# Mixer ends and the spread of the row scales in a three-block transformer kernel

## The chip, the cores and the metric

The kernel runs on one core of a Trainium2 chip, as one program and one launch. The metric is the device time of that launch in microseconds; before the change it is 1496.61 us, the median of three runs (1496.16 to 1496.88). The core has five engines with a queue of instructions each: TensorE (PE) multiplies matrices into PSUM banks, VectorE (DVE) and ScalarE (ACT) work elementwise and read PSUM, GpSimd (POOL) works elementwise on SBUF, and SyncE (SP) here only issues transfers.

## The reference, cut to what matters

256 tokens of width 1024 pass through two transformer layers of one kind and one of another, all in float32. Each of the first two layers is a feed-forward, a mixer (stick-breaking attention beside a convolution in the first layer, gated linear attention in the second) and another feed-forward; then comes a block with sparse attention, retention and a last feed-forward.

```python
for l in range(2):
    f = swiglu(rms_norm(h, g[0]), ffn1_w_in[l], ffn1_w_out[l])
    h = h + 0.5 * rms_norm(f, g[1])
    hn = rms_norm(h, g[2])
    m = even_mixer(hn, ...) if l % 2 == 0 else odd_mixer(hn, ...)
    h = h + rms_norm(m, g[3])
    f = swiglu(rms_norm(h, g[4]), ffn2_w_in[l], ffn2_w_out[l])
    h = h + 0.5 * rms_norm(f, g[5])
```

with `swiglu(x, w_in, w_out)`: split `x @ w_in` into `a` and `b`, then `(silu(a) * b) @ w_out`. A norm scales each token's row by the inverse root of its mean square, and each feature by a gain.

## The kernel before, in words

**Stages.** The program runs eight stages in a row: feed-forward, even mixer, feed-forward, feed-forward, odd mixer, feed-forward, the second block and its feed-forward. The loop over `i` (L1559) runs the first six. The 256 tokens are two tiles of 128 rows; `h` keeps both in SBUF. Between two stages stands `boundary` (L508): the last products of a stage for token tile 0, then for tile 1, and under those of tile 1 the next stage's input for tile 0 (transposes of `h` on TensorE, L409, then split columns `xh` and `xl`, L435 and L436). The transposes for tile 1 are put inside the next stage's first projection.

**Products in two parts.** Every float32 factor is split into a high half `hi` (a ScalarE copy, L248) and a low half `lo` (a subtraction, L249, mostly on VectorE), and each product is three matmuls: high by high (L271), low by high (L272) and high by low (L273). Nearly all weights come in chunks of 512 KB, in one fixed plan. `feed_dma` sends a chunk's transfer from SyncE into one of four `raw` buffers; `feed_cv` makes its halves. The transfer of chunk n + 4 goes into the buffer that the low half of chunk n sets free.

**What sets the order.** Nothing is scheduled: each engine works through its instructions in the order in which the code writes them. `nxt` hands out a chunk and first writes conversions ahead, up to one more than the chunks used, until they are `depth` ahead. `catch_up(n, lo_on)` writes up to n further conversions, with the low halves on VectorE or, with `pool`, on GpSimd. The tuples `PRE`, `PRT`, `PRF` and `CU` say how many of these stand at which place of `boundary`: the first two numbers ahead of tile 0's norm (on VectorE, on GpSimd), the third behind it (on GpSimd), then `CU[1]` behind tile 0's columns and `CU[2]` behind tile 0's scale (both on VectorE). `PRT` is for the two mixers, `PRF` for the four feed-forwards of the loop, `PRE` for the second block.

**Norms.** `add_normed` adds a stage's normed output to `h`: sums of squares on ScalarE (L359), then `rsqrt1` on 128x1 tiles of VectorE (L331 to L337), then for each half a gain (L374) and an addition (L380). `Lazy` keeps the next norm's row scales apart: `scale` makes them on GpSimd, and `rows` spreads them along the free axis: ScalarE puts each tile's scales on a diagonal `dg` (L448), TensorE multiplies by ones (L449), VectorE copies the result to `rb` (L451).

**A mixer's last projection.** `sproj_tail` makes it in four row blocks of the contraction: `part()` does the next one for both token tiles and both halves of the columns, `part(LO)` leaves out the two halves of tile 1, which `pieces()` then adds to the work of `boundary`. Each such piece is six matmuls.

**A feed-forward.** For 256 hidden features at a time (`j` from 0 to 10), `fa` and `fb` are projected, `sg = silu(fa * rb)` and `u = sg * fb` formed, `u` split into `hh` and `hl` (L550, L551), and the products with `fo` of the group before are added up (`fpart`). Group 0 has tokens on partitions, so that its `u0` is transposed (L739) in round `j = 1`, behind the spread.

Of the kernel before, what the change touches and what calls it, by code (L numbers as in the profile page):

```python
# [18 lines left out]
D = 1024  # L19
# [13 lines left out]
PRE = (1, 1, 2)  # L33
PRT = (0, 0, 2)
PRF = (0, 0, 2)
CT, CS = (2, 2), (0, 1)
CU = (2, 0, 1, 2)
# [143 lines left out]
class Norm:  # L181
    """a normalised activation on its way into the projections: split transposed columns and row scales"""
# [8 lines left out]
def block_kernel(ctx: ExitStack, tc: tile.TileContext, a: dict, out: bass.AP, upto: int = 99):  # L191
# [61 lines left out]
    def nxt(*names, ahead=True):  # L253
        """the next chunks; whatever uses the chunks before them is emitted already"""
        i = pos["use"]
        for d_, nm in enumerate(names):
            assert plan[i + d_][0] == nm, (plan[i + d_][0], nm)
        n = i + len(names)
        feed_cv(max(n, min(i - 1 + pos["depth"], pos["cv"] + len(names) + 1)) if ahead else n)
        pos["use"] += len(names)  # L260
        for _ in names:
            for f in list(side):
                f()
        r = [cv_t.pop(i + d_) for d_ in range(len(names))]
        return r if len(r) > 1 else r[0]

    def catch_up(n, lo_on=dve):
        feed_cv(min(pos["use"] - 1 + pos["depth"], pos["cv"] + n), lo_on)
# [56 lines left out]
    def rsqrt1(eng, ss, m, neps):  # L325
        """2^m / sqrt(ss[:, 0] + ss[:, 1] + neps)"""
        v = sm.tile([128, 1], F32, tag="rs_v", name="rs_v")
        vh = sm.tile([128, 1], F32, tag="rs_h", name="rs_h")
        y = sm.tile([128, 1], F32, tag="rs_y", name="rs_y")
        t = sm.tile([128, 1], F32, tag="rs_t", name="rs_t")  # L330
        eng.tensor_scalar(v, ss[:, 0:1], ss[:, 1:2], neps, op0=ALU.add, op1=ALU.add)  # L331
        eng.tensor_scalar(y.bitcast(I32), v.bitcast(I32), -0.5, float(MAGIC + (m << 23)), op0=ALU.mult, op1=ALU.add)
        if eng is dve:
            dve.tensor_scalar(vh, v, 0.5 * 4.0 ** -m, None, op0=ALU.mult)
            for _ in range(3):
                dve.scalar_tensor_tensor(t, in0=y, scalar=vh, in1=y, op0=ALU.mult, op1=ALU.mult)  # L336
                dve.scalar_tensor_tensor(y, in0=t, scalar=1.5, in1=y, op0=ALU.subtract, op1=ALU.mult, reverse0=True)  # L337
        else:
            pool.tensor_scalar(vh, v, -0.5 * 4.0 ** -m, None, op0=ALU.mult)
            for _ in range(3):  # L340
                pool.tensor_tensor(t, y, y, op=ALU.mult)
                pool.tensor_scalar(t, t, vh, 1.5, op0=ALU.mult, op1=ALU.add)  # L342
                pool.tensor_tensor(y, y, t, op=ALU.mult)
        return y

    def rsqrtn(v, n, big=False):
        """1 / sqrt(v), v: [128, n]"""
        mk = (lambda nm: s2([128, n], name=nm)) if big else (lambda nm: sm.tile([128, n], F32, tag=nm, name=nm))
        y, t = mk("rn_y"), mk("rn_t")
        dve.tensor_scalar(y.bitcast(I32), v.bitcast(I32), -0.5, float(MAGIC), op0=ALU.mult, op1=ALU.add)  # L350
        for _ in range(3):
            dve.scalar_tensor_tensor(t, in0=y, scalar=0.5, in1=y, op0=ALU.mult, op1=ALU.mult)
            dve.tensor_tensor(t, t, v, op=ALU.mult)
            dve.scalar_tensor_tensor(y, in0=t, scalar=1.5, in1=y, op0=ALU.subtract, op1=ALU.mult, reverse0=True)
        return y
# [11 lines left out]
    def add_normed(t, f, gb, m, rin=None):  # L367
        """h[:, t] += c * rms_norm(rin * f) * gb, c sqrt(D) = 2^m"""
# [24 lines left out]
    def add_gated(t, f, g):  # L393
        """h[:, t] += f * g"""
        for i in range(2):
            hv = h[:, t, i * 512:(i + 1) * 512]
            tm = s2([128, 512], name="tm")
            dve.tensor_tensor(tm, f[i], g[:, i * 512:(i + 1) * 512], op=ALU.mult)
            dve.tensor_tensor(hv, hv, tm, op=ALU.add)
            if i == 0:  # L400
                yield
# [9 lines left out]
    class Lazy:  # L411
        """x = h * r * g: columns of h * g, the row scales r apart"""
# [30 lines left out]
        def rows(self):  # L443
            """r along the free axis, in all partitions"""
            p = pb()
# [7 lines left out]
    class Shifted:  # L453
        """x = h * r * g + shift, whole"""
# [20 lines left out]
        def spread(self, t=0):  # L475
            """r along the free axis, in all partitions"""
# [30 lines left out]

    def boundary(pieces, fin, nz, pre=(0, 0, CU[0])):  # L508
        """the last products of a stage for token tile 0, then 1; the next stage's input for tile 0 under them"""
# [21 lines left out]
        catch_up(CU[1])  # L531
# [5 lines left out]
    def rows_T(t, src, xh, xl, halves=(0, 1)):  # L537
        """src [128 tokens, D] -> split transposed columns"""
# [15 lines left out]
    def wproj2(o, chs, x):  # L554
        """features on partitions, two tiles in one bank: o[:, i*256:] = (128 columns i of w)^T x^T"""
# [24 lines left out]
    def sproj(o, name, xh, xl, nk=8):  # L580
        """tokens on partitions: o(t) [128, 512] = x w, both token tiles chunk by chunk"""
# [5 lines left out]
    def sproj_ab(o, name, xh, xl, nk=8, mid=None):  # L587
        """the same, token tile 0 whole before 1"""
# [12 lines left out]
    def sproj_tail(name, xh, xl):  # L601
        """a projection to D columns, in four row blocks; part() does the next of them, pieces() the rest in boundary()"""
# [8 lines left out]
        def part(leave=()):  # L611
            """leave: (token tile, half) that wait for pieces()"""
# [47 lines left out]
    def ada_sum():  # L660
        """the four groups of 32 partitions together, and the columns to their places"""
# [8 lines left out]
    def gate_row(c0):  # L670
        """mod columns c0..c0+8 along the free axis, in all partitions: the tile and the work for its halves"""
# [12 lines left out]
    def ffn(nz, each=None):  # L684
# [45 lines left out]
        for j in range(1, NJ):  # L730
            if each and j > 1:
                each()
            pa = wp("fa", x)
            if j == 1:
                nz.rows()
# [6 lines left out]
            chb = nxt("fb", "fb")  # L742
# [6 lines left out]
            pb_ = pb()  # L749
            wproj2(pb_, chb, x)  # L750
# [24 lines left out]
    def even_mixer(nz):  # L775
# [91 lines left out]
        def logits(hp, pz, last):  # L867
            """masked, columns: keys 0..127 of all queries, then keys 128..255 of the later queries"""
# [108 lines left out]
        part()  # L977
        return f, pieces()

# [1 line left out]
    def odd_mixer(nz):  # L981
# [71 lines left out]
        def gate_sums():  # L1053
            """cs: sums within blocks of 64; last: the decay to the end of tile 0 and from the start of tile 1"""
# [12 lines left out]
        def halves(z, n):  # L1067
            """the lower and the upper blocks of n of each pair, all heads"""
# [8 lines left out]
        def decay(l):  # L1077
            """blocks of n = 64 >> l: the decay up to the end of the lower ones and from the start of the upper ones"""
# [117 lines left out]
    def second(nz):  # L1196
# [36 lines left out]
        def rope_in(p):  # L1233
            """p: [128 or 64, n, 256], two heads or one (then twice): a copy, and its turned features in their places"""
# [324 lines left out]
    for i in range(6):  # L1559
# [17 lines left out]
        boundary(pieces, lambda t: add_normed(t, f[t], gb, 5 if s == 1 else 4, rin[t]), nz, PRT if s == 1 else PRF)  # L1577
# [55 lines left out]
```

## Time and profile before

| | |
|---|---|
| device time, median of three runs | 1496.61 us |
| span of the profiled execution, first to last instruction | 1492.9 us |
| TensorE busy with matmuls | 1447.1 us, 97% |
| VectorE, ScalarE, GpSimd busy | 1031.9, 762.2 and 289.3 us |
| share of the longest chain on TensorE, VectorE, ScalarE | 79%, 11%, 4% |
| mean granted TensorE clock | 0.987 |

The execution whose trace is shown has 1492.9 us from its first to its last instruction; that is the span that all times below count from. TensorE is busy for 97% of it, so the rows that matter are the few in which it waits. In a timeline a row is start, length, engine, line, operation, output and inputs, shapes and count, and in brackets the idle time of the engine just before it and what ended that. Matmuls overlap, so a row's length is more than its share; the distance from one start to the next is what a product takes.

### The profile page before, as it was taken

What the parts mean: (1) busy time and instruction counts of PE and PEld (TensorE: products, weight loads), DVE (VectorE), ACT (ScalarE), POOL (GpSimd) and SP (SyncE); (2) the same over time, 40 slices, a digit from 0 to 9 for tenths busy, and PEclk for the clock granted to TensorE, in tenths of its full rate; (3) what the DMA queues carried; (4) which work ended last, traced back from release to release, by engine and by line L of the source; (5) the groups of instructions that cost most, each with busy time, mean ns of one, the idle gap of its engine ahead of it and who ended that gap; (6) DMA issues with size and microseconds to landing.
All of it is one profiled execution on the core that took longest, in us unless ns stands there. A gap on an engine that the chain in (4) does not pass through costs nothing.

```text
span 1492.9 us, 24718 instructions
## 1 busy us (share of the span) xinstructions
PE 1447.1 (97%) x9623; PEld 1319.9 (88%) x9623; DVE 1031.9 (69%) x1509; ACT 762.2 (51%) x1182; POOL 289.3 (19%) x429
## 2 busy tenths in 40 slices
PE   9999999689999999999999999999999999999997
PEld 8899989578999999999888799998898877899996
DVE  5777767986786667676677777765697865576543
ACT  5544356756444355443654455544643664564431
POOL 4000044823010040100423220101131131200001
PEclk9999999799999999999999999999999999999999
DMA  7887553235888558776542378854466464387640
GB/s 247 272 271 247 188 163 119 85 99 184 265 274 250 187 175 273 233 231 190 156 148 90 113 262 270 274 184 127 134 203 197 148 184 155 99 259 235 184 127 29
DMA packets 194950, 281.05 MB, mean 188 GB/s; under 512 B 12381, under 2 KB 148241, under 8 KB 194834
## 3 DMA queue, kind: packets, MB, share of 16 engines
q1 hardware_dynamic: 184386, 248.87, 53.0%
q0 software_dynamic: 10048, 30.03, 6.1%
q8 instruction: 75, 1.23, 0.3%
q10 hardware_dynamic: 400, 0.57, 0.1%
q14 instruction: 41, 0.34, 0.1%
HBM read 277.90 MB, written 1.05 MB: 187 GB/s over the span
## 4 chain that ended last, share of the span: by engine, by line
PE 79%; DVE 11%; ACT 4%; issue 3%; DMA 2%; POOL 2%; SPq 0%; DVEq 0%; ACTq 0%; POOLq 0%
PE pb L271 25%; PE pb L273 24%; PE pb L272 24%; DVE lo L249 3%; DMA raw<-in_ffn_w_in_dram 2%; DVE y L811 2%; ACT hi L248 2%; DVE yb L811 1%; POOL rs_t L342 1%; ACT sq L359 1%; DVE rs_t L336 1%; DVE rs_y L337 1%; PE pb L409 1%; ACT xh L435 1%; DVE xl L436 0%
## 5 line engine op out<-in xcount | busy, mean ns | idle before, releaser
L249 DVE TENSOR_TENSOR lo<-raw,hi 128x1024 fp32r<-128x1024 f32 (+1 forms) x457 | 544.4, 1218 | 239.7 <-ACT hi L248 205.0
L248 ACT ACTIVATE hi<-raw 128x1024 fp32r<-128x1024 f32 (+1 forms) x472 | 475.8, 1036 | 199.2 <-PE pb L273 69.9
L271 PE MATMUL pb<-xh,hi 128*128 128x256 f32 x1968 | 559.5, 284 | 2.8 <-DVE u L763 2.8
L272 PE MATMUL pb<-xl,hi 128*128 128x256 f32 x1968 | 557.7, 283 | 0.0
L273 PE MATMUL pb<-xh,lo 128*128 128x256 f32 x1968 | 557.7, 283 | 0.0
L271 PEld LDWEIGHTS pb<-xh,hi 128*128 128x128 f32 x1968 | 377.4, 192 | 6.2 <-issue 4.0
L272 PEld LDWEIGHTS pb<-xl,hi 128*128 128x128 f32 x1968 | 377.4, 192 | 2.0
L273 PEld LDWEIGHTS pb<-xh,lo 128*128 128x128 f32 x1968 | 377.3, 192 | 0.2
L271 PE MATMUL pb<-hi,hh 128*128 128x512 f32 x440 | 172.1, 391 | 0.0
L272 PE MATMUL pb<-lo,hh 128*128 128x512 f32 x440 | 171.8, 390 | 0.0
L273 PE MATMUL pb<-hi,hl 128*128 128x512 f32 x440 | 171.2, 389 | 0.0
L644 POOL DMA_DIRECT2D ada<-in_w_ada_dram x96 | 51.5, 539 | 443.3 <-PE pb L273 277.9
L550 ACT ACTIVATE hh<-u 128x512 fp32r<-128x512 f32 x50 | 31.6, 632 | 135.5 <-DVE u L763 135.5
L273 PEld LDWEIGHTS pb<-hi,hl 128*128 128x128 f32 x440 | 82.6, 188 | 17.6
L271 PEld LDWEIGHTS pb<-hi,hh 128*128 128x128 f32 x440 | 82.8, 188 | 15.7
L272 PEld LDWEIGHTS pb<-lo,hh 128*128 128x128 f32 x440 | 82.8, 188 | 15.4
L271 PE MATMUL pb<-hi,xh 128*128 128x512 f32 x224 | 90.7, 405 | 0.0
L273 PE MATMUL pb<-hi,xl 128*128 128x512 f32 x224 | 87.7, 392 | 0.0
L272 PE MATMUL pb<-lo,xh 128*128 128x512 f32 x224 | 87.5, 390 | 0.0
L249 POOL TENSOR_TENSOR lo<-raw,hi 128x1024 fp32r<-128x1024 f32 (+1 forms) x15 | 35.8, 2410 | 261.8 <-PE pb L272 187.3
L748 ACT ACTIVATE sg<-sg 128x512 f32<-128x512 f32 x40 | 25.3, 632 | 112.8 <-DVE sg L747 112.8
L649 DVE SCALAR_TENSOR_TENSOR adacc<-ada,sc,adacc 128x512 f32<-128x512 f32 x84 | 63.0, 750 | 2.0
(322 smaller groups left out, 1783.9 us busy)
## 6 DMA issues: line engine op xcount, KB each, us to landing
raw<-in_ffn_w_in_dram SPq DMA_DIRECT2D x176, 512.0 KB, 5.0
raw<-in_ffn_w_out_dram SPq DMA_DIRECT2D x88, 512.0 KB, 4.5
raw<-in_w_in_dram SPq DMA_DIRECT2D x56, 512.0 KB, 4.3
ada<-in_w_ada_dram POOLq DMA_DIRECT2D x96, 256.0 KB, 4.6
raw<-in_gla_w_in_dram SPq DMA_DIRECT2D x24, 512.0 KB, 4.2
raw<-in_w_ffn_gate_dram SPq DMA_DIRECT2D x22, 512.0 KB, 4.7
raw<-in_w_ffn_up_dram SPq DMA_DIRECT2D x22, 512.0 KB, 4.9
raw<-in_w_ffn_down_dram SPq DMA_DIRECT2D x22, 512.0 KB, 3.6
```

Source lines behind the costliest of these rows:

```text
L248: act.activation(hv, r, AF.Copy)
L249: lo_on.tensor_tensor(lv, r, hv, op=ALU.subtract)
L271: pe.matmul(o, lh, rh, start=start, stop=False)
L272: pe.matmul(o, lh, rl, start=False, stop=False)
L273: pe.matmul(o, ll, rh, start=False, stop=stop)
L336: dve.scalar_tensor_tensor(t, in0=y, scalar=vh, in1=y, op0=ALU.mult, op1=ALU.mult)
L337: dve.scalar_tensor_tensor(y, in0=t, scalar=1.5, in1=y, op0=ALU.subtract, op1=ALU.mult, reverse0=True)
L550: act.activation(hi, full, AF.Copy)
L644: pool.dma_start(t, w_ada[kt * 128:(kt + 1) * 128, cb * 512:(cb + 1) * 512])
L649: dve.scalar_tensor_tensor(ada["acc"], in0=t, scalar=sc[:, kt:kt + 1], in1=ada["acc"], op0=ALU.mult, op1=ALU.add)
L748: act.activation(sg, sg, AF.Silu)
L811: dve.scalar_tensor_tensor(o, in0=src, scalar=w, in1=o, op0=ALU.mult, op1=ALU.add)
```

## The change

Three things change. First, at the mixers' ends: the two conversions behind tile 0's norm had their low halves on GpSimd (`PRT`, third number). Now two conversions stand behind tile 0's columns with their low halves on VectorE (a new fourth number, which takes the place of `CU[1]`), and after the second mixer one more ahead of tile 0's norm on VectorE. `PRF` and `PRE` get a 0 there. Second, in the first mixer the second row block leaves two pieces to `boundary`, as the second mixer already does; with six pieces of tile 1 `boundary` puts the transposes two pieces ahead of the end, before it was one of four. Third, in round `j = 1` of every feed-forward the `fb` projection, with the conversions that its `nxt` writes, stands ahead of the spread and of the transposes of `u0`. Some comments and docstrings go as well.

```diff
-PRE = (1, 1, 2)
-PRT = (0, 0, 2)
-PRF = (0, 0, 2)
+PRE = (1, 1, 2, 0)
+PRT = ((0, 0, 0, 2), (1, 0, 0, 2))
+PRF = (0, 0, 2, 0)
-CU = (2, 0, 1, 2)
+CU = (0, 0, 1, 2)
...
-    def boundary(pieces, fin, nz, pre=(0, 0, CU[0])):
+    def boundary(pieces, fin, nz, pre):
...
         nz.evac(0)
-        catch_up(CU[1])
+        catch_up(pre[3])
...
             pa = wp("fa", x)
+            chb = nxt("fb", "fb")
+            pb_ = pb()
             if j == 1:
+                wproj2(pb_, chb, x)
                 nz.rows()
                 pr = pb()
...
-            chb = nxt("fb", "fb")
             sg = s2([128, 2, S], name="sg")
...
-            pb_ = pb()
-            wproj2(pb_, chb, x)
+            if j > 1:
+                wproj2(pb_, chb, x)
...
         conv_var()
-        part()
+        part(LO)
         return f, pieces()
...
-        boundary(pieces, lambda t: add_normed(...), nz, PRT if s == 1 else PRF)
+        boundary(pieces, lambda t: add_normed(...), nz, PRT[l] if s == 1 else PRF)
```

What this moves on the engines is seen in the order of their instructions. On ScalarE, from tile 1's scale in the feed-forward behind the first mixer, before:

```order
L359 ACTIVATE sq,ss<-h 128x512 x2
L248 ACTIVATE hi<-raw 128x1024 x2
L718 ACTIVATE sg<-pb,rs_y 128x256 x2
L248 ACTIVATE hi<-raw 128x1024 x3
L448 ACTIVATE dg<-ident,rs_y 128x128 x2
L550 ACTIVATE hh<-pb 128x512
```

and now:

```order
L718 ACTIVATE sg<-pb,rs_y 128x256 x2
L248 ACTIVATE hi<-raw 128x1024 x6
L448 ACTIVATE dg<-ident,rs_y 128x128 x2
L550 ACTIVATE hh<-pb 128x512
L750 ACTIVATE sg<-sg 128x512
```

The two `dg` stand behind six conversions instead of three. On VectorE, at the end of the first mixer, from tile 1's first gain (`tm`) over tile 0's split columns (`xl`) to tile 1's norm, before:

```order
L374 TENSOR_TENSOR tm<-pb,brow 128x512
L436 SCALAR_TENSOR_TENSOR xl<-pb,cols,xh 128x128 x8
L331 TENSOR_SCALAR rs_v<-ss 128x1
L332 TENSOR_SCALAR rs_y<-rs_v 128x1
L334 TENSOR_SCALAR rs_h<-rs_v 128x1
```

and now:

```order
L374 TENSOR_TENSOR tm<-pb,brow 128x512
L436 SCALAR_TENSOR_TENSOR xl<-pb,cols,xh 128x128 x8
L249 TENSOR_TENSOR lo<-raw,hi 128x1024 x2
L331 TENSOR_SCALAR rs_v<-ss 128x1
L332 TENSOR_SCALAR rs_y<-rs_v 128x1
```

Two low halves stand between the columns and the norm. On TensorE, round `j = 1` of the same feed-forward around the spread, before (the products ahead are the last of `fa`, those behind the first of `fb`):

```order
L273 MATMUL pb<-xh,lo 128x256
L449 MATMUL pb<-dg,ones 128x128 x2
L739 MATMUL pb<-ident,u 128x128 x4
L271 MATMUL pb<-xh,hi 128x256
L272 MATMUL pb<-xl,hi 128x256
```

and now (those ahead are the last of `fb`, those behind the first of `fo`):

```order
L273 MATMUL pb<-xh,lo 128x256
L449 MATMUL pb<-dg,ones 128x128 x2
L742 MATMUL pb<-ident,u 128x128 x4
L271 MATMUL pb<-hi,hh 128x512
L272 MATMUL pb<-lo,hh 128x512
```

The 48 products of `fb` have gone from behind the transposes to ahead of the spread, and what follows the transposes reads `hh`, which is made from them.

## Rows read from the trace of the kernel before

**Rows 1.** Waits of TensorE: line, waited for, us in total, times, longest.
```profile
PE pb L409 <- DVE h L380: 7.7, 6, 3.7
PE pb L449 <- ACT dg L448: 3.1, 4, 0.9
PE pb L271 <- DVE u L763: 2.8, 1, 2.8
```

**Rows 2.** Timeline, VectorE: first mixer's end and the feed-forward behind it.
```profile
324.41 0.43 DVE L551 TENSOR_TENSOR ml<-y,mh 128x256 fp32r<-128x256 f32 x1 [0.52 <-ACT mh L550]
...
330.31 2.43 DVE L336 SCALAR_TENSOR_TENSOR rs_t<-rs_y,rs_h 128x1 f32<-128x1 f32 x1
332.77 2.26 DVE L337 SCALAR_TENSOR_TENSOR rs_y<-rs_t,rs_y 128x1 f32<-128x1 f32 x1
335.06 0.22 DVE L336 SCALAR_TENSOR_TENSOR rs_t<-rs_y,rs_h 128x1 f32<-128x1 f32 x1
...
342.26 0.21 DVE L331 TENSOR_SCALAR rs_v<-ss 128x1 f32<-128x1 f32 x1 [0.23 <-ACT sq L359]
...
352.07 2.36 DVE L249 TENSOR_TENSOR lo<-raw,hi 128x1024 fp32r<-128x1024 f32 x2 [1.82 <-ACT hi L248]
...
362.22 0.69 DVE L551 TENSOR_TENSOR hl<-pb,hh 128x512 fp32r<-128x512 f32 x1 [0.32 <-ACT hh L550]
```

**Rows 3.** Timeline, GpSimd, first mixer's end.
```profile
330.32 4.70 POOL L249 TENSOR_TENSOR lo<-raw,hi 128x1024 fp32r<-128x1024 f32 x2 [25.57 <-DVE rs_y L337]
```

**Rows 4.** Timeline, TensorE: both mixers' ends and the feed-forwards' first products.
```profile
337.80 1.08 PE L409 MATMUL pb<-ident,h 128*128 128x128 f32 x4 [0.82 <-DVE h L380]
...
341.17 0.28 PE L702 MATMUL pb<-hi,xh 128*128 128x256 f32 x1
...
346.39 0.60 PE L409 MATMUL pb<-ident,h 128*128 128x128 f32 x4
...
846.10 1.03 PE L409 MATMUL pb<-ident,h 128*128 128x128 f32 x4 [2.35 <-DVE h L380]
...
857.00 0.60 PE L409 MATMUL pb<-ident,h 128*128 128x128 f32 x4
```

**Rows 5.** Windows, TensorE: stretch, us, busy (count), granted clock, DMA share, GB/s.
```profile
846.00:848.00 2.00, 1.45 (x6) 0.56 0.64 238
```

**Rows 6.** Timeline, ScalarE, round j = 1 of the first, third, fourth and sixth stage.
```profile
37.30 1.06 ACT L248 ACTIVATE hi<-raw 128x1024 fp32r<-128x1024 f32 x1 [3.31 <-DMA raw<-in_ffn_w_in_dram]
...
359.83 0.68 ACT L448 ACTIVATE dg<-ident,rs_y 128x128 f32<-128x128 f32 x2
361.58 0.60 ACT L550 ACTIVATE hh<-pb 128x512 fp32r<-128x512 f32 x1 [1.07 <-PE pb L739]
...
366.51 1.06 ACT L248 ACTIVATE hi<-raw 128x1024 fp32r<-128x1024 f32 x1 [0.42 <-DMA raw<-in_ffn_w_out_dram]
...
557.48 1.06 ACT L248 ACTIVATE hi<-raw 128x1024 fp32r<-128x1024 f32 x1 [0.49 <-DMA raw<-in_ffn_w_in_dram]
...
876.60 1.06 ACT L248 ACTIVATE hi<-raw 128x1024 fp32r<-128x1024 f32 x1 [0.43 <-DMA raw<-in_ffn_w_in_dram]
```

**Rows 7.** Timeline, TensorE, round j = 1 of the same four stages.
```profile
29.62 0.78 PE L449 MATMUL pb<-dg,ones 128*128 128x128 f32 x4 [0.71 <-ACT dg L448]
...
360.27 0.78 PE L449 MATMUL pb<-dg,ones 128*128 128x128 f32 x4 [0.81 <-ACT dg L448]
...
361.24 0.36 PE L271 MATMUL pb<-xh,hi 128*128 128x256 f32 x1
...
367.08 0.40 PE L271 MATMUL pb<-hi,hh 128*128 128x512 f32 x1
...
367.55 0.39 PE L273 MATMUL pb<-hi,hl 128*128 128x512 f32 x1
...
551.44 0.78 PE L449 MATMUL pb<-dg,ones 128*128 128x128 f32 x4 [0.86 <-ACT dg L448]
...
870.77 0.78 PE L449 MATMUL pb<-dg,ones 128*128 128x128 f32 x4 [0.71 <-ACT dg L448]
```

More of the change, by code (lines that the diff above doesn't have):

```diff
@@ L1576, in block_kernel @@
             nz = Shifted(A1, mod[:, 0:8], fill)
-        boundary(pieces, lambda t: add_normed(t, f[t], gb, 5 if s == 1 else 4, rin[t]), nz, PRT if s == 1 else PRF)
+        boundary(pieces, lambda t: add_normed(t, f[t], gb, 5 if s == 1 else 4, rin[t]), nz, PRT[l] if s == 1 else PRF)
         if upto == i:
```

## The prediction

> **What bounds the kernel now.** I read the waits of TensorE first, then the timeline around the waits that the change touches, engine by engine, and last the order of instructions, which says what stands where afterwards. The table above has TensorE busy for 1447.1 of 1492.9 us: a gain can only come out of its few gaps, and a new gap costs in full. Three entries of its waits belong to this change [rows 1]: transposes of `h` (L409) that wait for VectorE's addition, 7.7 us in six waits; the spread of the row scales (L449) that waits for ScalarE's `dg`, 3.1 us in four waits; and one wait of 2.8 us for `u` (L763), which stands at 68 us in the first feed-forward, where the chain of waits runs through weight transfers. The VectorE rows show why the longest of the first kind exists: two operations on 128x1 tiles take 2.43 and 2.26 us, while the next of the same kind takes 0.22 us [rows 2]; and GpSimd's two low halves fill just that stretch, 330.32 to 335.02 [rows 3]. After such a gap TensorE's clock is lower too: in the second mixer's end it idles 2.35 us [rows 4], and the granted clock of the next two microseconds is 0.56 [rows 5].
>
> **The mixer ends.** Three edits have no instruction behind them and cost nothing: `CU[0]` was read only as a default that every call overrides, and `PRE` and `PRF` get a fourth entry that equals the old `CU[1]`, 0. The rest goes in steps.
>
> Removed: the stalls of VectorE, 2.43 + 2.26 - 2 x 0.22 = 4.3 us [rows 2]. In the first mixer `h` of the first token tile is whole at about 337.7 (TensorE's second group of transposes starts on it at 337.80 [rows 4]), so it would be whole at 333.4. What is late next is TensorE itself. It does only half of the second row block ahead of the boundary, 12 products less, so it runs into the convolution's split columns, the last of which is written at 324.41 + 0.43 = 324.84 [rows 2]. Behind the product that needs it stand 12 products of the first tile and 24 of the second, each 0.235 us (367.08 and 367.55 are two products apart [rows 7]): 36 x 0.235 = 8.5, so 333.3. Both meet, and the transposes start without a wait at 333.4. A group of four took 1.08 us at the lowered clock [rows 4]; I give all eight as much at full clock, 334.4. Twelve products later the feed-forward starts at about 337.2 instead of 341.17 [rows 4]: 4.0 us early.
>
> Added: two conversions between the first tile's columns and the second tile's norm. Each is a high half on ScalarE (1.06 us [rows 6]) and a low half on VectorE (2.36 us for two [rows 2]). Queued behind them on VectorE are the second tile's norm and its additions, and for these TensorE waits inside the feed-forward's first projection (L409 again). Before, VectorE was done with the columns 0.23 us before the norm's first operation at 342.26 [rows 2], that is 3.15 us after the transposes ended at 338.88 [rows 4]. Now: 334.4 + 3.15 = 337.55 for the columns; ScalarE is through with its half of them about 0.4 us earlier, then 1.06 for a high half and 2.4 for both low halves: 340.6. From that first operation to the second group of transposes it was 346.39 - 342.26 = 4.13 us, a chain without slack, so that group stands at 344.7: of 4.0 us, **1.7 us** stay. TensorE idles about 2 us in the feed-forward for it.
>
> The second mixer has the same pair of stalls. TensorE was ready at 846.10 - 2.35 = 843.75 [rows 4], and `h` comes 4.3 us earlier, so it doesn't wait. Transposes end at 844.8, columns at 847.95, and 847.55 + 1.06 + 2.4 = 851.0 for the low halves; 4.13 us later is 855.1 against 857.00 [rows 4]: **1.9 us**. The extra conversion ahead of that tile's sums of squares falls where ScalarE and VectorE wait for TensorE; I cost it at nothing, and without that cover it is one conversion, 1.1 us. Together -3.6 us. Whether the two new gaps of about 2 us lower the clock, no row says; one that does costs about 0.9 us (0.44 of two microseconds [rows 5]). I take +0.6 for both.
>
> The Trainium skill, SBUF — State Buffer, section Who interferes with whom, says that a VectorE instruction with two SBUF inputs is blocked wholly by a GpSimd instruction that reads SBUF, and the other way round. By that the 4.3 us go, as the rows have it; but the rule speaks against the change as well, since the two low halves then block GpSimd's own norm of the first tile from VectorE. That norm is wanted only when the feed-forward has its first projection done, so I cost it at nothing.
>
> **The feed-forward.** The new order sends `fb` ahead of the spread, and with it three conversions ahead of `dg` on ScalarE. These wait for weights: in the third stage the last of them starts at 366.51, behind a wait for its transfer, and runs 1.06 us [rows 6]. Their buffers are freed by low halves that keep their place, so they land no earlier. `dg` follows at 367.57 instead of 359.83, and TensorE's spread 0.44 us after it (360.27 - 359.83 [rows 6, 7]), at 368.01: 7.74 us later than before. TensorE is through with `fb` well before that: it reaches it 0.81 us before the old start of the spread and takes 5.84 us (361.24 to 367.08 [rows 7]), so it waits 7.74 + 0.81 - 5.84 = 2.7 us. It also loses what covered the next step. `hh` (0.60) and `hl` (0.69) are made from the transposes, and the products of `fo` now follow at once: `hl` ends at 362.22 + 0.69 = 362.91, 2.64 us after the spread's start [rows 2, 6, 7]. Before, the first product that needs `hl` came 367.55 - 360.27 = 7.28 us after the spread, behind `fb` [rows 7]. So that product moves by the delay of the spread less 7.28 - 2.64 = 4.64:
>
> - third stage: 7.74 - 4.64 = **+3.1**
> - fourth stage: last conversion at 557.48, spread at 558.98 against 551.44: 7.54 - 4.64 = **+2.9** [rows 6, 7]
> - sixth stage: 876.60, spread at 878.10 against 870.77: **+2.7** [rows 6, 7]
> - first stage: 37.30, spread at 38.80 against 29.62: +4.5 [rows 6, 7]. There the 2.8 us at 68 us [rows 1] are slack of TensorE, so **+1.7** remain; the bounds are nothing, if the transfers alone still set that point, and the whole 4.5
> - last feed-forward: no `dg`, only the lost cover: 5.84 - 4.64 = **+1.2**
>
> Sum +11.6. All of it lies on TensorE, which has no further wait in these stages [rows 1], so only the first stage's slack gives anything back. The new waits are 2.7, 2.5, 2.2 and 4.1 us; after 2.35 the clock fell [rows 4, 5], so I add 0.9 for each of the first two and 0.6 for the third, +2.4; in the first stage the low clock after 68 us is exchanged for one at 39.
>
> **Sum.** -3.6 + 0.6 + 11.6 + 2.4 = +11.0 us, on a span of 1492.9: 1503.9. The runs' median is 1496.61, 3.7 us around the span; with these, **1507.6 us**.
>
> **Rivals.**
> 1. *The seams keep all they gain.* If the two conversions didn't hold the second tile, both seams would keep 4.0 and about 4.5 us: -8.5 + 11.6, with no clock loss, is +3.1, 1499.7. For it: the feed-forward really starts that early. Against: the order puts both low halves ahead of the norm, and that chain had no slack.
> 2. *The weights are there in time* (not slower). The mechanism is the landing of the third conversion's transfer in the feed-forward. If it landed 2.7 us earlier, at 363.8, the spread would find `dg` ready; then the 3.1 us of old waits go [rows 1], and five times the wait for `hl` comes (362.91 less the end of the transposes, which is 0.09 before `hh` at 361.58, less two products: 0.95), 4.8: +1.7, and with -3.6 the sum is -1.9, 1494.7. Together with the first rival it would be -6.8, 1489.8. It decides from about 3 us earlier, in all four stages. Against: in all four ScalarE waits there for a transfer [rows 6].
>  The Trainium skill, SBUF — State Buffer, section Summary, gives about 358 GB/s from HBM; an estimate from it is 1.5 us for the 512 KB of a chunk, and by that this rival would hold. No run here shows a chunk moved alone, and these rows show ScalarE waiting for one among others.
> 3. *The clock falls at every new gap, and the seams give nothing.* +11.6 + 2.8 (the first stage without its slack) + 4 x 0.9, and 0 from the seams: +18.0, 1514.6. For it: several short gaps follow each other in the first mixer's end and in the feed-forward's first round.
> 4. *The change has no effect on the spread*: only if `dg` kept its place, and the order shows it behind three more conversions.
>
> **From this the numbers.** Forecast 0.72, rival 1 0.10, rival 2 0.06, rival 3 0.12, rival 4 nothing. The forecast's own range is +6 to +15. The range runs from 1501.0 to 1512.5: it leaves out rival 2, part of rival 1 and the far end of rival 3. A measurement of this kernel tells 0.2%, 3 us, from no change: faster 0.04 (rival 2 with part of rival 1), within 0.08 (half of rival 1, half of rival 2), slower 0.88.
>
> **What would show it.** Right: the waits of TensorE list L449 behind `dg` with about 11 us in four waits instead of 3.1, and new waits of some 0.7 us for `hh` at the first products of `fo` in all five feed-forwards; no VectorE operation on 128x1 tiles above 0.3 us at the mixer ends; the L409 waits moved from the first tile to the second, near 2 us each. Wrong: L449 waits under 1 us, so that the conversions did not hold `dg`; or the transposes still waiting for the first tile, so that GpSimd was not what stalled VectorE.

## The result and the profile after

Four runs of the changed kernel took 1506.67 to 1511.54 us, median 1509.17, against 1496.38 (1495.85 to 1496.88) for the kernel before: ratio 1.0083, 95% interval 1.0071 to 1.0095. The profiled execution took 1508.55 us with a span of 1506.8, 13.9 more than before. The forecast was 1507.6 us, with a range of 1501.0 to 1512.5.

The waits of TensorE in the changed kernel (line, releaser; total us, times, longest), answering [rows 1]; code lines behind the change in the feed-forward lie two or three higher:

```profile
PE pb L449 <- ACT dg L448: 11.9, 4, 3.5
PE pb L409 <- DVE h L380: 4.0, 3, 1.9
PE pb L271 <- ACT hh L550: 3.6, 5, 0.7
PE pb L271 <- ACT mh L550: 1.3, 1, 1.3
```

The spread's wait has grown from 3.1 to 11.9 us, the wait for `h` has halved, and five waits for `hh` are new.

VectorE at the first mixer's end, answering [rows 2]. GpSimd has nothing to do there until 341.18:

```profile
330.04 0.22 DVE L336 SCALAR_TENSOR_TENSOR rs_t<-rs_y,rs_h 128x1 f32<-128x1 f32 x1
330.29 0.16 DVE L337 SCALAR_TENSOR_TENSOR rs_y<-rs_t,rs_y 128x1 f32<-128x1 f32 x1
...
338.37 2.36 DVE L249 TENSOR_TENSOR lo<-raw,hi 128x1024 fp32r<-128x1024 f32 x2 [0.59 <-ACT hi L248]
340.64 0.21 DVE L331 TENSOR_SCALAR rs_v<-ss 128x1 f32<-128x1 f32 x1
```
```profile
341.18 0.30 POOL L331 TENSOR_SCALAR rs_v<-ss 128x1 f32<-128x1 f32 x1 [36.25 <-ACT sq L359]
```

The two long operations are gone, and the two moved low halves stand ahead of the second tile's norm, which starts at 340.64 (forecast 340.6). TensorE there and at the second mixer's end, answering [rows 4]:

```profile
321.78 0.50 PE L271 MATMUL pb<-hi,mh 128*128 128x512 f32 x1 [1.25 <-ACT mh L550]
...
333.59 1.04 PE L409 MATMUL pb<-ident,h 128*128 128x128 f32 x8
...
343.33 0.66 PE L409 MATMUL pb<-ident,h 128*128 128x128 f32 x4 [1.90 <-DVE h L380]
344.72 0.66 PE L409 MATMUL pb<-ident,h 128*128 128x128 f32 x4
...
862.16 0.66 PE L409 MATMUL pb<-ident,h 128*128 128x128 f32 x4 [1.90 <-DVE h L380]
863.55 0.66 PE L409 MATMUL pb<-ident,h 128*128 128x128 f32 x4
```

The first tile's eight transposes run without a wait, the second tile's wait 1.90 us at both seams. The feed-forward's spread on ScalarE and TensorE in the third stage, answering [rows 6, 7]:

```profile
355.40 3.89 ACT L248 ACTIVATE hi<-raw 128x1024 fp32r<-128x1024 f32 x4
363.48 2.00 ACT L248 ACTIVATE hi<-raw 128x1024 fp32r<-128x1024 f32 x2 [4.18 <-DMA raw<-in_ffn_w_in_dram]
365.38 0.68 ACT L448 ACTIVATE dg<-ident,rs_y 128x128 f32<-128x128 f32 x2
367.14 0.60 ACT L550 ACTIVATE hh<-pb 128x512 fp32r<-128x512 f32 x1 [1.07 <-PE pb L742]
```
```profile
365.82 0.78 PE L449 MATMUL pb<-dg,ones 128*128 128x128 f32 x4 [2.22 <-ACT dg L448]
366.44 0.60 PE L742 MATMUL pb<-ident,u 128*128 128x128 f32 x4
367.79 0.80 PE L271 MATMUL pb<-hi,hh 128*128 128x512 f32 x1 [0.75 <-ACT hh L550]
...
563.56 0.78 PE L449 MATMUL pb<-dg,ones 128*128 128x128 f32 x4 [3.53 <-ACT dg L448]
...
885.02 0.78 PE L449 MATMUL pb<-dg,ones 128*128 128x128 f32 x4 [2.60 <-ACT dg L448]
```

`dg` is the next thing that ScalarE does after the sixth conversion, and the last two conversions have waited for a transfer. The last two rows are the spread in the fourth and the sixth stage. Windows of the changed kernel (stretch, us, then busy time with counts of TensorE, its weight loads, VectorE, ScalarE and GpSimd, then granted clock, DMA share, GB/s), answering [rows 5]: the two new gaps at the seams, then what follows the spread's wait in the third, the fourth and the sixth stage:

```profile
343.00:349.00 6.00, 5.65 (x46) 5.45 (x47) 5.11 (x12) 3.33 (x11) 3.35 (x7) 1.00 0.55 180
862.00:868.00 6.00, 5.82 (x48) 5.62 (x49) 4.94 (x12) 3.49 (x11) 3.19 (x7) 1.00 0.52 177
...
366.00:374.00 8.00, 7.25 (x23) 5.62 (x24) 5.79 (x7) 5.01 (x7) 0.54 (x1) 0.57 0.62 193
...
563.00:571.00 8.00, 6.76 (x26) 5.39 (x27) 5.48 (x7) 5.63 (x9) 0.54 (x1) 0.79 0.50 169
...
885.00:893.00 8.00, 7.23 (x22) 5.57 (x23) 5.54 (x7) 5.28 (x7) 0.00 (x0) 0.57 0.52 153
```

After the gaps of 1.90 us TensorE keeps its upper level of 2.4 GHz. After the spread's wait the mean over eight microseconds is 0.57 in the third and the sixth stage, so most of it runs at 1.2 GHz, and 0.79 in the fourth.

### The profile page after: what moved, and what is told of

The parts are those of the page before. It is cut to its first block, busy times and chain, and to the rows that moved or that the text cites. A ratio compares the mean times of both kernels' runs of the same rounds, so it can differ in the third digit from the quotient of the medians.

```text
span 1506.8 us, 24705 instructions
## 1 busy us (share of the span) xinstructions
PE 1451.0 (96%) x9623; PEld 1319.7 (88%) x9623; DVE 1028.9 (68%) x1513; ACT 762.5 (51%) x1182; POOL 278.3 (18%) x425
## 3 DMA queue, kind: packets, MB, share of 16 engines
HBM read 277.90 MB, written 1.05 MB: 185 GB/s over the span
## 4 chain that ended last, share of the span: by engine, by line
PE 79%; DVE 10%; ACT 4%; issue 3%; DMA 2%; POOL 2%; SPq 0%; DVEq 0%; ACTq 0%; POOLq 0%
PE pb L271 25%; PE pb L273 25%; PE pb L272 25%; DVE lo L249 3%; DMA raw<-in_ffn_w_in_dram 2%; DVE y L813 1%; DVE yb L813 1%; ACT hi L248 1%; POOL rs_t L342 1%; ACT xh L435 1%; ACT sq L359 1%; DVE xl L436 0%; DVE ex L1077 0%; PE pb L409 0%; DMA raw<-in_w_in_dram 0%
## 5 line engine op out<-in xcount | busy, mean ns | idle before, releaser
L271 PE MATMUL pb<-hi,hh 128*128 128x512 f32 x440 | 176.6, 401 | 3.6 <-ACT hh L550 3.6
L272 PE MATMUL pb<-lo,hh 128*128 128x512 f32 x440 | 174.9, 397 | 0.0
L273 PE MATMUL pb<-hi,hl 128*128 128x512 f32 x440 | 174.3, 396 | 0.0
L550 ACT ACTIVATE hh<-u 128x512 fp32r<-128x512 f32 x50 | 31.6, 632 | 149.3 <-DVE u L765 149.3
L249 POOL TENSOR_TENSOR lo<-raw,hi 128x1024 fp32r<-128x1024 f32 (+1 forms) x11 | 26.4, 2424 | 223.2 <-PE pb L272 189.3
```

Source lines behind the costliest of these rows:

```text
L249: lo_on.tensor_tensor(lv, r, hv, op=ALU.subtract)
L271: pe.matmul(o, lh, rh, start=start, stop=False)
L272: pe.matmul(o, lh, rl, start=False, stop=False)
L273: pe.matmul(o, ll, rh, start=False, stop=stop)
L550: act.activation(hi, full, AF.Copy)
```

## Where the time went, stage by stage

The transposes of `h` (L409) mark the boundaries between stages. This table, worked out from their starts in each kernel's profile, gives each stage's length less that of the kernel before, in us. A feed-forward runs from the second tile's last transposes to the next boundary's first ones (the first one from its own first transposes, the last one to the end of the span). A mixer runs from there to the second tile's last transposes at its end, so that its seam is in it, and the second block from the boundary ahead of it to the one behind it. The kernels from `e1` on are the experiments below.

```
                     first  even  third  fourth  odd   sixth  second  last
                     FF     mixer FF     FF      mixer FF     block   FF
after                 0.0   -1.9   5.4    5.1   -2.2    5.8    0.4    1.1
e1_ff_only            3.0    1.3   4.1    3.8    1.7    5.6    0.3    1.2
e2_ends_only          3.9   -1.9   0.1    0.0   -2.2    0.2    0.4   -0.1
e3_dg_first           0.1   -1.8   3.3    3.6   -0.6    2.0    0.4    1.2
e4_fill               2.7   -1.2   3.3    2.9   -0.7    3.0    0.5    1.2
e6_dg_early           0.3    0.7  -1.2   -1.2   -0.1    0.3    0.2   -0.1
e7_both               1.4   -4.1   3.0   -1.2   -4.6   -0.3    0.0   -0.1
e8_ends_whole         2.1   -1.4   0.6    0.0   -0.7    0.2    0.6   -0.1
e9_fb_later_conv     -3.7   -1.9   1.9    0.0   -2.2    0.3    0.5    1.2
e10_ends_later_conv   2.6   -4.1   3.7    0.0   -3.0    3.8    0.5   -0.1
e11_both_no_conv     -1.6   -4.1  -1.2   -1.2   -4.5   -0.1    0.4    1.4
e12_odd_later        -0.1   -1.8   0.3   -1.2   -2.9   -0.8    1.1   -0.1
```

The first feed-forward scatters between -3.7 and +3.9 from profile to profile, also where no edit touches it (`e2_ends_only` +3.9); one profile says nothing on it. The feed-forwards behind it repeat within about 0.6 us where nothing is changed in them. The mixers do not always: in `e1_ff_only`, which leaves both as they were, they are 1.3 and 1.7 us longer, and the same odd mixer gives 2.2 us in three kernels and 0.6 or 0.7 in three others. One reason is TensorE's clock behind a gap (last section). In the row of the changed kernel the seams give 4.1 us, and the third, fourth and sixth stage take 16.2.

## The experiments

**The two parts alone.** `e1_ff_only` is the kernel before with this edit alone, `e2_ends_only` the changed kernel without it:

```
             pa = wp("fa", x)
+            chb = nxt("fb", "fb")
+            pb_ = pb()
             if j == 1:
+                wproj2(pb_, chb, x)
                 nz.rows()
...
-            chb = nxt("fb", "fb")
...
-            pb_ = pb()
-            wproj2(pb_, chb, x)
+            if j > 1:
+                wproj2(pb_, chb, x)
```

> The kernel before with the feed-forward part alone. Read stage by stage, the changed kernel's trace gives the seams -4.1 us (1.85 and 2.25 between the mixers' last products and the second token tile's transposes) and the rest +18.0 us. Theory (the two parts are independent): before + 18 us, 1514.5 us, with L449 waiting for dg about 12 us in four waits. Rival (the low clock after the spread's wait comes from the two-microsecond gaps at the seams some 20 us earlier, which this kernel has not): about 3 us less in the third and in the sixth stage, 1508.5 us.

> The kernel before with the mixer ends alone. Theory (independent parts, two gaps of 1.9 us for h that leave the clock alone): -1.85 and -2.25, 1492.4 us; L449 waits for dg as before, 3 us in four waits. Rival A (what the seams gain is lost again at the next wait for weights in the feed-forward): 1496.5 us. Rival B (the seams could keep all that VectorE's stalls cost): -8.5, 1488 us.

`e1_ff_only` took 1514.88 us against 1496.93 for the kernel before on the same chip, ratio 1.0117 (1.0104 to 1.0130): 18 us. `e2_ends_only` took 1493.47, ratio 0.9971 (0.9960 to 0.9983): 2.5 to 6.0 us faster. Together that is +14.5 us, near the +12.8 of the whole change. The waits of the one and of the other:

```profile
PE pb L449 <- ACT dg L448: 11.7, 4, 4.8
PE pb L409 <- DVE h L380: 7.9, 6, 3.7
```
```profile
PE pb L409 <- DVE h L380: 4.1, 4, 1.9
PE pb L449 <- ACT dg L448: 3.3, 4, 0.9
```

Each part brings its own waits and leaves the other's as they were: the mixer ends are a gain, and the loss is the feed-forward's. The low clock behind the spread does not need the new gaps at the seams. In `e1_ff_only`, which has the old gaps there, the sixth stage loses 5.6 us, and in the fourth stage, which follows no mixer, the clock falls in both kernels. In its third and fourth stage `e1_ff_only` loses about 1.2 us less each than the changed kernel, and the traces show where. In the third the clock behind the spread is less low (0.79 over the eight microseconds from 372, against 0.57). In the fourth the last two conversions waited 3.29 and 0.81 us for their transfers instead of 3.66 and 1.71.

**The clock apart from the wait.** `e4_fill` puts products whose results are not used where TensorE waits for `dg`:

```
         def rows(self, idle=None):
             p = pb()
+            if idle:
+                for _ in range(18):
+                    pe.matmul(p[:, :S], *idle, start=True, stop=True)
...
-                nz.rows()
+                nz.rows((chb[0][0][:, 0, :128], x.h[:, 0]))
```

> The changed kernel with 18 products whose results are not used (128x256, 2.2 us in all at full clock) on TensorE between fb and the spread, where it waits for dg. The wait for dg keeps its end, so no time is gained by order; only the clock can move. Theory (the gap of 2.2 to 3.5 us at that place lets the clock fall, and 6 us at half speed cost about 3 us): the gap becomes 0 to 1.3 us, the clock stays up, -2.7 to -2.9 in each of three stages, 1501 us. Rival A (the clock falls at the run of short gaps, the later one for hh included, or for another reason): 1509 us. Rival B (added products run past the time at which dg is there): some stages up to 1 us later, 1510 us.

It took 1504.93 us, ratio to before 1.0051 (1.0038 to 1.0065), 4.2 us under the changed kernel's median. Its windows of the third, fourth and sixth stage:

```profile
368.00:376.00 8.00, 7.25 (x45) 6.05 (x44) 4.84 (x6) 5.51 (x9) 0.54 (x1) 1.00 0.82 271
563.00:571.00 8.00, 6.99 (x37) 5.44 (x36) 4.76 (x7) 5.63 (x9) 0.54 (x1) 1.00 0.70 240
885.00:893.00 8.00, 7.03 (x36) 5.42 (x35) 5.66 (x7) 5.57 (x9) 0.00 (x0) 1.00 0.52 165
```

Now the clock stays up in all three, and they lose 3.3, 2.9 and 3.0 us instead of 5.4, 5.1 and 5.8, together 7.0 less. Not all of that is the clock, because the spread starts at another place of the stage. From the second tile's last transposes to the spread the changed kernel takes 21.11, 22.41 and 21.48 us, `e4_fill` 21.73, 21.37 and 21.27. From the spread to the next boundary the changed kernel takes 165.95, 164.46 and 166.18 us, `e4_fill` 163.27, 163.28 and 163.67. So the low clock behind the spread costs 2.7, 1.2 and 2.5 us, together 6.4, less than the 8.1 to 8.7 expected. In the fourth stage another 1.0 us comes from the last two conversions, which waited 0.5 and 0.6 us longer for their transfers in the changed kernel. The total falls by less than 7.0: the profile of `e4_fill` has 2.7 us more in the first feed-forward and 0.6 and 1.6 more in the two mixers, and the mixers' part is the clock as well (last section). Rival A falls. Rival B holds for the third stage, where the spread follows the added products without a wait and comes 0.6 us later than in the changed kernel.

**`dg` ahead of `fb`'s conversions.** `e3_dg_first` makes both `dg` after `fa`'s conversions, ahead of those that come with `fb`; everything else is the changed kernel's:

```
             pa = wp("fa", x)
+            if j == 1 and not nz.early:
+                nz.diag()                # the two dg activations of rows()
             chb = nxt("fb", "fb")
```

> The changed kernel with dg issued on ScalarE ahead of fb's three conversions; the products of fb stay ahead of the spread. Theory (dg queued behind conversions that wait for transfers is the cost): the waits of L449 fall under 1 us each; hh is still behind the conversions, so the first products of fo wait for it 1 to 2.2 us in three stages; each of the third, fourth and sixth stage gains 1.7 us directly, and the clock stays up in at least two of them, 2.7 us each: 1509.2 - 5.1 - 5.4 = 1498.7 us (1497 to 1502). Rival (the products of fb ahead of the spread are what costs, since they covered hh and hl): 1507 to 1509 us.

It took 1503.35 us, ratio to before 1.0041 (1.0029 to 1.0053): 5.8 us better than the changed kernel and not 10.5. As expected L449 is no longer among the waits, and `hh` is in its place (its line L550 is L557 where `diag` is in the kernel):

```profile
367.64 0.50 PE L271 MATMUL pb<-hi,hh 128*128 128x512 f32 x1 [1.54 <-ACT hh L557]
...
560.80 0.50 PE L271 MATMUL pb<-hi,hh 128*128 128x512 f32 x1 [1.66 <-ACT hh L557]
...
883.10 0.50 PE L271 MATMUL pb<-hi,hh 128*128 128x512 f32 x1 [1.44 <-ACT hh L557]
```

Of the 4.7 us that are missing, about 3 lie elsewhere in the profiled execution: 1.3 us ahead of the third stage's spread, where the transposes behind the seam's gap take 1.11 us instead of 0.66 and the granted clock is 0.72 over the six microseconds from 344, and 1.6 us in the odd mixer (last section). The rest is a direct gain that was overestimated: `hh` stands behind the same three conversions, the products behind `hh` then waited up to 1.0 us for `hl`, and in the third stage the last conversion began at 366.05, 1.6 us later than in the changed kernel. So `dg`'s place is not the whole price. This run could not tell the rest of the queue from the order of the products.

**The conversions apart from the products.** `e9_fb_later_conv` keeps the new order on TensorE and only puts the three conversions off:

```
-            chb = nxt("fb", "fb")
+            chb = nxt("fb", "fb", ahead=j > 1)
```

> The changed kernel, with the products of fb still ahead of the spread, but without the three conversions that were issued with them: ScalarE has dg and hh directly behind the conversions of fa, and the three are made up at later chunks. Theory (the three conversions ahead of dg and hh, the last of which waits for its transfer, are the whole price of the feed-forward's part): no wait of L449 above 0.3 us, hh waited for by 0.7 us as the transposes have no cover, so per feed-forward +0.4 to +1.2 us against the kernel before; with the seams' -4.1 the sum is 1494.5 to 1496.5 us. Rival A (the order of TensorE's products costs by itself, since fb no longer covers the spread, hh and hl): 1503 us or more. Rival B (conversions made up later leave a later chunk of fa unconverted): the waits move to L271 behind lo or hi, and the time lies between, 1498 to 1503 us.

It took 1491.72 us against 1497.84, ratio 0.9965 (0.9951 to 0.9980): with one argument the changed kernel goes from 0.8% slower to 0.35% faster. Its waits:

```profile
PE pb L409 <- DVE h L380: 4.1, 4, 1.9
PE pb L271 <- ACT hh L550: 3.8, 5, 1.0
```

No wait of L449 is listed, the waits for `hh` are the lost cover, and the third, fourth and sixth stage lose 1.9, 0.0 and 0.3 us instead of 16.2 in all. Of the 1.9, 1.4 lie ahead of the spread, behind the seam's gap, where the clock fell in this execution (0.72 over the six microseconds from 341). Rival A falls: in these stages the order of the products costs at most 0.5 us by itself. In the last feed-forward, which has no `dg`, the lost cover costs 1.2 us as in the changed kernel. Of rival B's waits one of 0.7 us is listed. The time is below the range expected, and in its profile what exceeds it lies in the first feed-forward (-3.7), so I claim only the direction.

**The two pieces left to the seam.** `e8_ends_whole` is `e2_ends_only` with `part()` in place of `part(LO)` in the first mixer.

> The kernel before with the mixer ends, but without the two pieces left to the first mixer's seam: TensorE does the whole second row block ahead of the boundary. The trace of the changed kernel has TensorE waiting 1.25 us for the convolution's columns at 321.8 and finding h of the first tile ready at 333.6. Theory (the stall of VectorE decides at that seam, and the two pieces only change which wait is seen): the wait for the columns goes, one of about as much for h comes before the first tile's transposes, and the seam from the mixer's last wait to the second tile's transposes is within 0.5 us of the ends alone. Rival (the 12 products are the cover that makes the seam work): the transposes come 2.8 us later, and the second tile's with them.

It took 1495.17 us, ratio 0.9989 (0.9975 to 1.0003), which is not clear of no change. TensorE at its first seam:

```profile
334.69 0.60 PE L409 MATMUL pb<-ident,h 128*128 128x128 f32 x4
335.74 0.63 PE L409 MATMUL pb<-ident,h 128*128 128x128 f32 x4 [0.44 <-DVE h L380]
...
345.06 1.11 PE L409 MATMUL pb<-ident,h 128*128 128x128 f32 x4 [3.25 <-DVE h L380]
```

The mixer with its seam is 1.4 us shorter than before instead of 1.9, and the third stage behind it starts more slowly (0.6 instead of 0.1): the pieces are worth 0.5 to 1 us in this profile, and the rival's 2.8 falls. The wait for the first tile's `h` is 0.44 us, and the wait on the second tile is 3.25 instead of 1.90; its transposes take 1.11 us instead of 0.66, and the granted clock is 0.57 over the eight microseconds from 344.

**What held the second tile.** `e10_ends_later_conv` is `e2_ends_only` with the seam's two conversions behind the second tile's columns:

```
         nz.evac(0)
-        catch_up(pre[3])
...
                 nz.evac(1)
                 nz.scale(1)
-                catch_up(CU[3])
+                catch_up(CU[3] + nz.more)      # nz.more = pre[3]
```

> The kernel before with the mixer ends, the two conversions of each seam moved behind the second token tile's columns, inside the feed-forward's first projection. Theory (these two conversions hold the second tile's addition, and nothing else): the two waits of 1.9 us for h on the second tile go, the seams keep 4.0 and 4.3 us instead of 1.85 and 2.2, 1493.5 - 4 = 1489.5 us. Rival (their transfers are then issued some 8 us later and the feed-forward waits for weights): 1493 us or more, with L449 waiting over 1 us in the third and sixth stage.

It took 1497.60 us, ratio 0.9993 (0.9979 to 1.0006): no change in the sum, and both sides were right about their part. The even mixer gains 4.1 us instead of 1.9, nearly the 4.3 that VectorE's stalls had cost, so the two low halves did hold the second tile. But the third and the sixth stage give 3.7 and 3.8 us back. Of these, 2.2 and 2.3 lie at the wait that the rival named, and 1.5 each behind it, where the granted clock is 0.79 over eight microseconds:

```profile
PE pb L449 <- ACT dg L448: 7.6, 4, 3.0
```

**Towards a version that beats both.** `e6_dg_early` is the kernel before with `dg` made ahead of `fa`'s first conversions (`nz.diag()` ahead of `pa = wp("fa", x)`), `e7_both` has this and the edit of `e10_ends_later_conv`.

> The kernel before with dg issued ahead of fa's three conversions, so that it is there when the first products of fa end. Theory (the 3.1 us in four waits of L449 are dg's place behind the conversions): the waits go, 0.8 us in each of the third, fourth and sixth stage, 1496.5 - 2.4 = 1494 us. Rival (dg ahead of the conversions delays these by 0.7 us and with them the next transfers, and the wait turns up at hh): 1496.5 us, no change.

> Both moves together on the kernel before: mixer ends with the two conversions inside the feed-forward's first projection, and dg ahead of fa's conversions, the spread ahead of fb's products as before. If each does what its theory says: -7 - 2.4, 1487 us. If both rivals hold: 1493 to 1496.5 us.

They took 1495.30 us, ratio 0.9986 (0.9976 to 0.9997), and 1486.93, ratio 0.9932 (0.9916 to 0.9948). `dg` early takes 1.2 us out of the third and the fourth stage, more than the 0.8 expected, and nothing out of the sixth; the kernel comes out about 2 us faster, within reach of both sides. That `e7_both` met its 1487 is partly luck: the mixers give 8.7 us, more than the 7 counted, and the third stage loses 3.0 us where 0.8 were to be gained, at a place that nobody named, a later chunk:

```profile
399.51 0.50 PE L271 MATMUL pb<-hi,hh 128*128 128x512 f32 x1 [2.00 <-ACT hh L557]
```

Two ways to mend that: `e11_both_no_conv` also puts off `fa`'s three conversions in the first round (`nxt("fa", "fa", ahead=j > 1)`), `e12_odd_later` leaves the first seam's two conversions at the seam.

> The kernel of both moves (1486.9 us) without the three conversions of fa's first call, so that dg and hh stand directly behind the first projection on ScalarE. Theory (a conversion is only in the way of dg and hh and can be made up later): the waits for hh go, and the third stage returns from +3.0 to about -1.2 us against before: 1482.5 us. Rival (every conversion that is put off puts off a transfer, and the first third of a feed-forward is short of transfers): the wait turns up at a later chunk, 1487 us or more.

> The kernel of both moves, with the two conversions of the first mixer's seam back at the seam, as in the changed kernel, and only those of the second mixer's seam inside the feed-forward. Theory (stages are independent: in the third stage the later transfers cost 4.2 us more than the seam's 2.3 us bring, in the sixth less): the even seam -1.85 instead of -4.1, the third stage -1.2 instead of +3.0, 1486.9 - 1.9 = 1485 us. Rival (the loss in the third stage is from dg ahead of the conversions): 1489 us.

`e11_both_no_conv` took 1483.85 us against 1496.68, ratio 0.9918 (0.9897 to 0.9938), the fastest of all: the third stage comes to -1.2 as its theory said. No wait of the spread for `dg` is left in its list, 0.2 us for `h` and 0.4 for `hh`; new are small ones for weights:

```profile
PE pb L271 <- ACT hi L248: 1.8, 2, 1.6
PE pb L273 <- DVE lo L249: 1.5, 2, 0.8
```

`e12_odd_later` took 1489.66, ratio 0.9953 (0.9939 to 0.9967), 4.7 us above its theory and near the rival's 1489. Yet its rival falls: `dg` is ahead of the conversions here, and from the spread on the third stage takes 167.62 us, as in `e6_dg_early` and `e11_both_no_conv`. It is at +0.3 and not at -1.2 because of 1.4 us ahead of the spread, where the granted clock is 0.72 over the six microseconds from 344, behind the seam's gap of 1.90. Another 1.6 us lie in the odd mixer, which is that much longer than in `e7_both` and has a granted clock of 0.77 from 775 to 780, around a gap of 2.05 us (last section). The other 1.7 us stay open.

## Why the prediction held

By its steps, with the terms of the sum:

- **VectorE's stall** went as said: 0.22 and 0.16 us in place of 2.43 and 2.26 [rows 2]. The rule of the Trainium skill on the ports that VectorE and GpSimd share (SBUF — State Buffer, Who interferes with whom) agrees: with GpSimd idle there is nothing left to block.
- **The seams.** Transposes were forecast for 333.4 and the second tile's for 344.7; they came at 333.59 and 344.72, the gaps are 1.90 us, and the stages give 1.9 and 2.2 us for a forecast of 1.7 and 1.9. `e10_ends_later_conv` confirms the reason. The clock term there, +0.6, was nothing in this execution. The extra conversion of the second mixer was costed at nothing; no run takes it out alone.
- **The spread's delay in the feed-forward.** The forecast was 3.1, 2.9 and 2.7 us in the third, fourth and sixth stage and 1.2 in the last. What the changed kernel loses there without the low clock is 2.7, 3.9, 3.3 and 1.1 (from the stretches measured with `e4_fill`). Putting the conversions off takes nearly all of it away in these three (`e9_fb_later_conv`). The waits were forecast as 2.7, 2.5, 2.2 and, in the first stage, 4.1; 2.22, 3.53, 2.60 and 3.52 were measured. In the fourth stage the last conversion waited 1.71 us for its transfer, against 0.49 before [rows 6]; the forecast had it start as late as before and no later. Why the transfer came later, no run tells.
- **The first feed-forward**, +1.7, came out at 0.0, within its bounds of 0 and 4.5; the scatter of this stage forbids more.
- **The clock behind the spread** is the term that was mis-sized: +2.4 forecast, 6.4 measured. I took the loss after a gap from one window of two microseconds [rows 5], 0.9 us. The same trace had more to give: over six microseconds the mean is 0.72 (row below), which is 1.7 us. Behind the spread the low level lasted longer still in the third and the sixth stage (0.57 over eight microseconds). It did not in the fourth (0.79), whose wait was the longest of the three; why, no run tells.

```profile
846.00:852.00 6.00, 5.45 (x22) 0.72 0.21 79
```

So +11.0 on the span became +13.9: 4.0 more for the clock behind the spread, 1.2 for the spread's delay, nearly all in the fourth stage, and 0.4 in the second block, less 1.7 in the first stage and 0.6 and 0.5 at the seams. The steps were right, but terms that were 5.6 us too low and terms that were 2.8 too high partly cancel, so part of the closeness is luck. Rival 3 was half true: the clock fell at the long gaps, but not at the seams, and these gave what they should. Rival 1 fell, as the order had it (`e10_ends_later_conv` shows what it would have given). Rival 2, weights in time, did not occur: ScalarE waited 4.18 us for them in the third stage.

## What to carry to other kernels

When work is moved on one engine, ask which instructions come with it on the others: here the helper that hands out the weights also queues three conversions, and these, not the products that moved, cost 14 of the 16 us in three stages, with the low clock that followed; one argument took that away. A short operation that the busiest engine waits for belongs ahead of anything that waits for a transfer, but what it pushes back may be waited for later, as in `e7_both`. And a new gap on TensorE is to be priced with the clock that may follow it, from the longest low stretch that the trace shows, not from the first two microseconds.

## What was not expected of the hardware

The clock after a gap near two microseconds goes either way. Ahead of the odd mixer's sums of the decay TensorE waits 2.05 us in each of these profiles; in the changed kernel and in `e4_fill` the same eight products, and the windows that follow, then read so:

```profile
787.91 1.13 PE L1101 MATMUL pb<-last 128*128 128x128 f32 x8 [2.05 <-DVE last L1077]
```
```profile
789.00:791.00 2.00, 2.00 (x11) 1.60 (x10) 2.00 (x3) 1.14 (x2) 0.00 (x0) 1.00 0.00 0
```
```profile
787.45 2.04 PE L1105 MATMUL pb<-last 128*128 128x128 f32 x8 [2.05 <-DVE last L1081]
```
```profile
789.00:791.00 2.00, 2.00 (x8) 1.67 (x7) 2.00 (x4) 0.60 (x1) 0.00 (x0) 0.54 0.16 13
```

The odd mixer is 1.6 us longer in the second, with nothing changed there; those eight products are also long in `e3_dg_first`, `e8_ends_whole` and `e10_ends_later_conv` (1.82, 1.49, 1.64). The seams' gaps are of this kind too. Six profiles have one of 1.9 us at the first seam. In `e3_dg_first`, `e4_fill`, `e9_fb_later_conv` and `e12_odd_later` the clock fell behind it, and the second tile's transposes take 1.05 to 1.11 us instead of 0.66; in the changed kernel and in `e2_ends_only` it did not. One that falls costs 1.3 to 1.4 us, by what lies ahead of the third stage's spread in three of them. So the +0.6 of the prediction was not wrong in kind, it did not happen in the profiled execution. Such gaps are one reason for runs of one kernel that lie microseconds apart; how much of that they explain was not tried.

VectorE also holds GpSimd up, but off the path: in the first tile's norm on GpSimd one operation on 128x1 takes 1.12 us where its equal takes 0.27, while VectorE makes a low half.

```profile
343.43 0.27 POOL L342 TENSOR_SCALAR rs_t<-rs_t,rs_h 128x1 f32<-128x1 f32 x1
...
344.81 1.12 POOL L342 TENSOR_SCALAR rs_t<-rs_t,rs_h 128x1 f32<-128x1 f32 x1
```
```profile
344.58 1.22 DVE L249 TENSOR_TENSOR lo<-raw,hi 128x1024 fp32r<-128x1024 f32 x1
```

It ends 0.13 us after that low half. This is the other direction of the rule named above. The low half is that of the conversion behind the first tile's scale, which the kernel before has as well (1.11 us at 346.39 there). The two moved ones, which the prediction expected to block this norm, are over at 340.73, before it starts at 341.18. TensorE waits for none of it.
